# Eight ring places for the first weight granules, and S5's input weights asked for behind the sixth pair of modulation tiles

## The chip, the cores and the metric

One NeuronCore of a Trainium2 chip runs the whole program in one launch. The metric is the device time of one execution in microseconds (us).

## The reference

Two layers of a hybrid backbone over 256 context tokens and 256 latent tokens of width 1024, all in float32. What matters here is the beginning of each layer:

```python
def hybrid_layer(x, xc, c, c_ctx, p, cos, sin, ctx_out):
    mods = [m[:, None, :] for m in adaln(c, p)]     # silu(c) @ w_ada + b_ada, split in 6
    cmods = adaln(c_ctx, p)
    h = modulate(rmsnorm(x, p['norm1_g']), mods[0], mods[1])
    hc = modulate(rmsnorm(xc, p['norm1_g']), cmods[0], cmods[1])
    ua, ub, uatt, us5, ug = split_sections(h @ p['w_in'])
    ...
```

Four token mixers (RWKV-7, GLA, windowed attention, S5) follow, then their merge, the output projection, a second norm and a mixture of experts. `w_ada` is 1024 x 6144 per layer, `w_in` 1024 x 6688.

## The kernel before, in words

Weights come from HBM in *granules*: one granule is 128 partitions x 1024 float32, 512 KB, and holds eight 128 x 128 blocks. `gload` (L229) asks for one on SyncE's DMA queue and puts it in the next place of a ring, `self.ring`. In the first layer the ring has two places at first (pool `wp`) and four (with pool `wa`) while the modulation is computed. A place is asked for again only when its reader is done. `gsplit` (L239) loads a granule and splits it in two parts for the matmuls of high precision: ScalarE rounds it to float32r (tile `gs`), VectorE subtracts to get the rest (a second `gs`). `rowpair` (L266) does this for the two granules of S5's input weights.

The program is written as a sequence, and a scheduler deals its instructions out to the engines at build time; on each engine they then run in that order. So moving a call in the source can move the order on all engines for some distance around it.

In the first layer (`layer`, L1881) the beginning is this: x is loaded (`xi`, two requests of 1 MB), S5's small parameters (`s5_load`) on ScalarE's queue, S5's input weights by `rowpair` (L1916), and the norm (`norm1`): ScalarE squares and sums, VectorE works out the reciprocal root (tile `n`), both scale `xi`, TensorE transposes it into PSUM (`pb`), and ScalarE and VectorE copy it to `xr`. Then for each of eight column blocks k:

- `adaln` multiplies two granules of `w_ada` (k and 8 + k) with the conditioning vector (TensorE, `ada`), and VectorE adds the result to `mods`;
- `modcols` picks rows of `mods` out by a small matmul (`mps`), and VectorE makes scale and shift of it (`mc`, two instructions);
- `modulate` scales the two halves of `xr` (VectorE), ScalarE rounds to `hh`, VectorE subtracts to `hl`.

`s5` then begins with the projection of all eight blocks (matmuls `pa<-gs,hh` and `pa<-gs,hl`, 96 for the four quarters of time). The modulation columns 16 to 47 are multiplied later between other work, by `early`. PSUM bank A, which `ada` and `pa` share, has two buffers, so each waits for VectorE's use of the one before the last.

The tiles `yT` (L1895) hold the outputs of the four mixers, 128 x 1024 float32 each in the first layer; they are first written far into the layer. `kd` in DRAM is zeroed in part by two small DMAs (`zr`).

Of the kernel before, what the change touches and what calls it, by code (L numbers as in the profile page):

```python
# [9 lines left out]
F32 = mybir.dt.float32  # L10
# [167 lines left out]
class Net:  # L178
# [50 lines left out]
    def gload(self, src, pool=None):  # L229

        k, n = src.shape[1:]
        if pool is None:
            pool = self.ring[self.ri % len(self.ring)]
            self.ri += 1
        v = pool.tile([128, 1024], F32, tag="g", name="g")[:, 0:k * n].rearrange("p (k n) -> p k n", k=k)
        self.nc.sync.dma_start(v, src)
        return v

# [1642 lines left out]
    def layer(self, l, lo):  # L1881
        nc, tc, io = self.nc, self.tc, self.io
        nt = (512 - lo) // 128
        front = self.psum(f"pf{l}", A=2, X=1, B0=2, B1=2, C=1)
        self.ws = {s: ExitStack() for s in ("left", "right")}
        self.slots, self.early = [], []
        fs, hs, rs, bs = (ExitStack() for _ in range(4))

        def pool(es, name, side="left", bufs=1):
            return es.enter_context(tc.tile_pool(name=f"{name}{l}", bufs=bufs, side=side, reuse_waits="tile"))  # L1890
        wp = pool(fs, "wp", "right", 2)
        self.ring = [wp] * 2
        F = pool(fs, "F", "right")
        H = pool(hs, "H", "right")
        yT = [H.tile([128, 2, 512 - lo], F32, name=f"yT{i}") for i in range(4)]  # L1895
        h = [H.tile([128, 8, 512], F32R, name=n) for n in ("hh", "hl")]
        rm, p3, p4 = pool(rs, "rm"), pool(bs, "p3"), pool(bs, "p4")
        wx = pool(bs, "wx")

        self.mres = rm.tile([128, 512], F32, name="mres")  # L1900
        nc.gpsimd.memset(self.mres, 1.0)
        nc.gpsimd.memset(self.mres.rearrange("p (j t) -> p j t", t=64)[:, :, 0:1], 0.0)

        self.gp = [(F, f"a{i}") for i in range(4)] if l == 0 else [(self.xp, "x0"), (self.xp, "x1"), (F, "a0"), (F, "a1")]
        with ExitStack() as ns:
            tp = pool(ns, "n")
            mc = tp.tile([128, 2, 2, 8], F32, name="mc")
            mps = self.pc("mps")
            if l == 0:
                x = tp.tile([128, 4, D], F32, name="xi")  # L1910
                for s in range(2):
                    nc.sync.dma_start(x[:, 2 * s:2 * s + 2, :], io["x"][:, 2 * s:2 * s + 2, :])
                s5p = self.s5_load(l, p3)
                xr = tp.tile([128, 8, 512], F32, name="xr")
                xs = [x[:, t, :] for t in range(4)]
                s5w = self.rowpair(io["w_in_s5"][l, 0])  # L1916
                self.norm1(xs, xs, tp, lambda k, ps: (nc.vector.tensor_copy if k % 2 else nc.scalar.copy)(xr[:, k, :], ps))
                self.ring = self.ring + [pool(ns, "wa", bufs=2)] * 2
                for k in range(8):
                    self.adaln(0, [k, 8 + k])  # L1920
                    self.modcols(l, [k], mc, mps)
                    self.modulate(k, mc, h, xr[:, k, :], xr[:, k, :])
                self.ring = self.ring[0:2]
            else:
                self.modcols(l, range(8), mc, mps)
                s5p = self.s5_load(l, p3)
                gp, self.gp = self.gp, [(tp, "g0"), (F, "a0"), (tp, "g1"), (F, "a1")]
                s5w = self.rowpair(io["w_in_s5"][l, 0])
                self.gp = gp
                xn = [tp.tile([128, D], F32, name=f"xn{t}") for t in range(4)]  # L1930
                self.norm1(self.x, xn, tp, lambda k, ps: self.modulate(
                    k, mc, h, ps, tp.tile([128, 512], F32, tag="xm", bufs=2, name="xm")))
            s5p = self.s5_head(l, s5p, p3)
        todo = [(0, j) for j in range(16, 48)] + [(1, j) for j in range(16)] if l == 0 else [(1, j) for j in range(16, 48)]

        def some(n, bank="A"):
            for _ in range(min(n, len(todo))):
                a, j = todo.pop(0)
                self.adaln(a, [j], wx, bank)
        NB, C1, C2 = 24, 0, 3  # L1940

        def early(n):
            for _ in range(n):
                a, j = todo.pop(0)
                self.adaln(a, [j], wx, "X")
        early(32 if l else 0)
        self.bt = "B1"
        self.s5(l, h, s5w, yT[3], lo, p3, s5p)
        self.bt = "B0"
        early(0 if l else NB)  # L1950
        with ExitStack() as es:
            self.gla(l, h, yT[1], lo, pool(es, "p2"))
        st = self.rwkv_in(l, h, lo, rm, p4, lambda: None)
        us = ExitStack()
        up = pool(us, "up", "right")
        self.rwkv_first(l, st, up)
        with ExitStack() as es:
            self.attn(l, h, yT[2], lo, pool(es, "p1"))
        bs.close()
        m = 1024 // (512 - lo)  # L1960
        acc = [F.tile([128, m, 512 - lo], F32, tag=f"a{i}", name="acc") for i in range(8 // m)]
        acc = [a[:, i, :] for a in acc for i in range(m)]
        with ExitStack() as es:
            p0, p = pool(es, "p0"), pool(es, "p5")
            self.gp = [(p, f"g{i}") for i in (0, 1, 2, 2)] if l == 0 else self.gp[0:2] + [(p, "g0"), (p, "g1")]
            self.rwkv_units(l, st, yT[0], p0, p, 4 if l else 3)
            for n, i in enumerate((1, 3, 2)):
                self.merge(l, i, h, yT[i], acc, lo, n == 0, p, lambda: some(C1), self.pa if l == 0 else None)
        us.close()
        rs.close()  # L1970
        if l == 0:
            self.xp = self.xs.enter_context(tc.tile_pool(name="xp", bufs=1, reuse_waits="tile"))
        self.bt = "B0"
        wo = pool(self.ws["left"], "wo", bufs=4)
        self.eopen(l, "left", EB[l][0])
        with ExitStack() as es:
            p = pool(es, "p6")
            if l == 0:
                wx = pool(es, "wy", bufs=2)
            self.gp = [(p, f"g{i}") for i in range(4)] if l == 0 else self.gp[0:2] + [(p, "g0"), (p, "g1")]  # L1980
            self.merge(l, 0, h, yT[0], acc, lo, False, p, lambda: some(C2, "B1"), self.pb)
        if l == 0:
            self.xload()
        w = [self.blocks([self.wtile(io["w_out"][l, n, :, k:k + 4], wo) for k in (0, 4)]) for n in range(2)]
        self.eahead(l)
        hs.close()
        with ExitStack() as es:
            mo = pool(es, "mo")
            ex = self.tail(l, lo, acc, mo, w)
            fs.close()  # L1990
            front.__exit__(None, None, None)
            self.eopen(l, "right", EB[l][1])
            self.eahead(l)
            self.slots += [wo] * 4
            self.moe(l, lo, ex)
        self.ws["right"].close()
        self.ws["left"].close()
# [22 lines left out]
```

## Time and profile before

| | |
|---|---|
| median of 3 runs | 2438.41 us (2432.42 to 2440.38) |
| the profiled execution | 2436.24 us, its span 2434.5 us |
| TensorE busy | 2233.6 us (92% of the span) |
| VectorE busy | 1220.8 us (50%) |
| ScalarE busy | 657.7 us (27%) |
| mean granted TensorE clock | 0.959 of full speed |

The span runs from the first to the last instruction; the execution's own time has 1.7 us around it. Times in the rows below are counted from the span's start. A line number such as L272 can be that of a helper that records every matmul, so rows are told apart by the names of the tiles, written as result <- inputs.

### The profile page before, as it was taken

How to read it: one execution, taken by the hardware profiler on the slowest of the kernel's cores; microseconds unless marked ns; L12 is line 12 of the kernel's file. 1: busy time of each engine (PE TensorE's matmuls, PEld its weight loads, DVE VectorE, ACT ScalarE, POOL GpSimd, SP SyncE). 2: the span in 40 equal slices, each digit the busy share in tenths (PEclk: the TensorE clock that was granted, in tenths of full speed). 3: DMA queues.
4: the chain of work that ended last, by engine and by line, in shares of the span. 5: the costliest groups of instructions: out<-in, count | busy, mean ns of one | idle time of the engine just before them, and what ended most of it. 6: DMA issues, size and time to landing. Idle time of an engine off the chain costs nothing. (4 is left out here: it accounts for less than half of the span.)

```text
span 2434.5 us, 38729 instructions
## 1 busy us (share of the span) xinstructions
PE 2233.6 (92%) x15351; PEld 1302.5 (54%) x15351; DVE 1220.8 (50%) x3229; ACT 657.7 (27%) x1217; POOL 316.0 (13%) x351
## 2 busy tenths in 40 slices
PE   5999989999999799999999799999999799999996
PEld 4876757677764333333333486767778433333332
DVE  6685567754433454332333668858755432222222
ACT  3254443322211111111111325543333111111111
POOL 0000000000000043323333100100000012222211
PEclk9997989999999799999999799989999799999998
DMA  7342111115470799999997244412228499999994
GB/s 249 124 137 78 62 44 41 51 58 185 147 242 20 274 419 417 380 399 381 378 379 305 77 152 157 136 59 78 65 91 302 180 375 418 419 419 419 419 419 206
DMA packets 149436, 557.42 MB, mean 229 GB/s; under 512 B 38484, under 2 KB 69588, under 8 KB 98820
## 3 DMA queue, kind: packets, MB, share of 16 engines
q1 hardware_dynamic: 139088, 542.66, 58.2%
q10 hardware_dynamic: 5556, 5.94, 0.8%
q0 software_dynamic: 4608, 6.30, 0.8%
q8 instruction: 124, 2.03, 0.3%
q14 instruction: 60, 0.49, 0.1%
HBM read 558.56 MB, written 6.75 MB: 232 GB/s over the span
## 5 line engine op out<-in xcount | busy, mean ns | idle before, releaser
L272 PE MATMUL pa<-hh,gs 128*128 128x512 f32 (+2 forms) x1440 | 421.3, 367 | 9.2 <-ACT sg L275 5.2
L272 PEld LDWEIGHTS pa<-hh,gs 128*128 128x128 f32 (+1 forms) x1440 | 254.4, 190 | 68.4 <-issue 15.1
L272 PE MATMUL pd<-w,hT 128*64 128x512 f32 x1024 | 278.3, 599 | 1.4 <-ACT hT L275 1.4
L272 PE MATMUL pgate<-w,xT 128*64 128x512 f32 x1024 | 262.6, 602 | 0.0
L272 PE MATMUL pa<-hl,gs 128*128 128x512 f32 (+2 forms) x720 | 254.8, 367 | 0.0
L272 PE MATMUL pup<-w,xT 128*64 128x512 f32 x1024 | 250.5, 592 | 0.0
L278 POOL TENSOR_TENSOR ta<-ta,mb 128x512 f32<-128x512 f32 x93 | 125.0, 1351 | 726.9 <-ACT ta L275 726.8
L278 DVE TENSOR_TENSOR gs<-g,gs 128x1024 fp32r<-128x1024 f32 (+1 forms) x106 | 128.2, 1211 | 111.2 <-PE pa L272 82.5
L275 ACT ACTIVATE gs<-g 128x1024 fp32r<-128x1024 f32 (+1 forms) x106 | 110.5, 1045 | 190.9 <-PE pa L272 140.0
L272 PEld LDWEIGHTS pup<-w,xT 128*64 128x64 f32 x1024 | 81.3, 137 | 146.5 <-issue 144.8
L272 PE MATMUL py<-yp,oT 128*128 128x512 f32 x384 | 128.3, 437 | 31.2 <-ACT ta L275 23.1
L272 PEld LDWEIGHTS pd<-w,hT 128*64 128x64 f32 x1024 | 81.7, 136 | 138.1 <-issue 130.3
L272 PEld LDWEIGHTS pgate<-w,xT 128*64 128x64 f32 x1024 | 75.7, 138 | 148.9 <-issue 137.5
L272 PEld LDWEIGHTS pa<-hl,gs 128*128 128x128 f32 (+1 forms) x720 | 138.0, 192 | 27.2 <-issue 7.9
L272 PEld LDWEIGHTS py<-yp,oT 128*128 128x128 f32 x384 | 62.1, 190 | 122.2 <-ACT ta L275 44.5
L288 DVE SCALAR_TENSOR_TENSOR hd<-hd,pgate 128x512 f32<-128x512 f32 x32 | 22.0, 688 | 208.0 <-ACT hd L275 207.9
L278 POOL TENSOR_TENSOR x<-x,ta 128x512 f32<-128x512 f32 x93 | 123.8, 1337 | 3.8
L278 DVE TENSOR_TENSOR tm<-py,mb 128x512 f32<-128x512 f32 x99 | 66.7, 687 | 88.3 <-PE py L272 88.3
L272 PE MATMUL pa<-gs,hh 128*128 128x256 f32 x480 | 107.6, 319 | 2.4 <-DVE gs L278 1.8
L1660 DVE TENSOR_TENSOR hd<-hd,pup 128x512 f32<-128x512 f32 x32 | 22.0, 687 | 174.4 <-PE pup L272 174.4
L275 ACT ACTIVATE yp<-pd,at 128x512 fp32r<-128x512 f32 x64 | 44.0, 688 | 241.7 <-PE pd L272 241.7
L288 DVE SCALAR_TENSOR_TENSOR yp<-pd,at,yp 128x512 fp32r<-128x512 f32 x64 | 47.7, 745 | 122.6 <-ACT yp L275 122.6
(505 smaller groups left out, 3408.1 us busy)
## 6 DMA issues: line engine op xcount, KB each, us to landing
w<-in_w_g SPq DMA_DIRECT2D x128, 1024.0 KB, 11.6
w<-in_w_d SPq DMA_DIRECT2D x128, 1024.0 KB, 13.3
w<-in_w_u SPq DMA_DIRECT2D x128, 1024.0 KB, 12.1
g<-in_w_ada SPq DMA_DIRECT2D x96, 512.0 KB, 3.9
g<-in_w_in_gate SPq DMA_DIRECT2D x64, 512.0 KB, 3.8
g<-in_w_in_rwkv SPq DMA_DIRECT2D x16, 512.0 KB, 3.9
wb<-in_w_branch SPq DMA_DIRECT2D x64, 128.0 KB, 3.6
w<-in_w_out SPq DMA_DIRECT2D x8, 1024.0 KB, 6.4
```

Of the source, the lines that this page charges most:

```text
L272: self.nc.tensor.matmul(out, lhsT, rhs, start=start, stop=stop, skip_group_check=True)
L275: self.nc.scalar.activation(out, in_, f, **kw)
L278: (eng or self.nc.vector).tensor_tensor(out, a, b, op)
L288: self.nc.vector.scalar_tensor_tensor(out, a, s, b, op0=op0, op1=op1)
L1660: last = nc.vector.tensor_tensor(hd, hd, pu, OP.mult).ins
```

## The change

Granules can now be put in a place of any pool and tag. While the first layer's modulation is computed the ring has eight places, the four of before and four in pool H with the tags y0 to y3. The four `yT` tiles are made after `s5_head`, with the same tags, so each takes the memory of one of these places. S5's input weights are asked for inside the loop, ahead of k = 6, where twelve modulation granules have been asked for.

```diff
--- before.py
+++ after.py
@@ -232,7 +232,8 @@
         if pool is None:
             pool = self.ring[self.ri % len(self.ring)]
             self.ri += 1
-        v = pool.tile([128, 1024], F32, tag="g", name="g")[:, 0:k * n].rearrange("p (k n) -> p k n", k=k)
+        pool, tag = pool if isinstance(pool, tuple) else (pool, "g")
+        v = pool.tile([128, 1024], F32, tag=tag, name="g")[:, 0:k * n].rearrange("p (k n) -> p k n", k=k)
         self.nc.sync.dma_start(v, src)
         return v
 
@@ -1892,7 +1893,6 @@
         self.ring = [wp] * 2
         F = pool(fs, "F", "right")
         H = pool(hs, "H", "right")
-        yT = [H.tile([128, 2, 512 - lo], F32, name=f"yT{i}") for i in range(4)]
         h = [H.tile([128, 8, 512], F32R, name=n) for n in ("hh", "hl")]
         rm, p3, p4 = pool(rs, "rm"), pool(bs, "p3"), pool(bs, "p4")
         wx = pool(bs, "wx")
@@ -1913,10 +1913,12 @@
                 s5p = self.s5_load(l, p3)
                 xr = tp.tile([128, 8, 512], F32, name="xr")
                 xs = [x[:, t, :] for t in range(4)]
-                s5w = self.rowpair(io["w_in_s5"][l, 0])
                 self.norm1(xs, xs, tp, lambda k, ps: (nc.vector.tensor_copy if k % 2 else nc.scalar.copy)(xr[:, k, :], ps))
-                self.ring = self.ring + [pool(ns, "wa", bufs=2)] * 2
+
+                self.ring = self.ring + [pool(ns, "wa", bufs=2)] * 2 + [(H, f"y{i}") for i in range(4)]
                 for k in range(8):
+                    if k == 6:
+                        s5w = self.rowpair(io["w_in_s5"][l, 0])
                     self.adaln(0, [k, 8 + k])
                     self.modcols(l, [k], mc, mps)
                     self.modulate(k, mc, h, xr[:, k, :], xr[:, k, :])
@@ -1931,6 +1933,8 @@
                 self.norm1(self.x, xn, tp, lambda k, ps: self.modulate(
                     k, mc, h, ps, tp.tile([128, 512], F32, tag="xm", bufs=2, name="xm")))
             s5p = self.s5_head(l, s5p, p3)
+        yT = [H.tile([128, 2 * (512 - lo)], F32, tag=f"y{i}", name=f"yT{i}").rearrange("p (z n) -> p z n", z=2)
+              for i in range(4)]
         todo = [(0, j) for j in range(16, 48)] + [(1, j) for j in range(16)] if l == 0 else [(1, j) for j in range(16, 48)]
 
         def some(n, bank="A"):
```

SyncE's queue (`SP`) at the start of the program. Names: `xi` is x, `in_w_in_s` S5's input weights, `in_w_ada` the modulation weights, `zr` the zeros for `kd`, `in_w_in_gla` and its like the weights of GLA. Before:

```order
L1912 DMA xi<-in_x 128x2048 x2
L236 DMA g<-in_w_in_s 128x1024 x2
L236 DMA g<-in_w_ada 128x1024 x2
L1102 DMA kd<-zr 112x256
L236 DMA g<-in_w_ada 128x1024 x6
L1103 DMA kd<-zr 112x256
L236 DMA g<-in_w_ada 128x1024 x10
L236 DMA g<-in_w_in_glaa 128x256
```

And now:

```order
L1912 DMA xi<-in_x 128x2048 x2
L237 DMA g<-in_w_ada 128x1024 x12
L237 DMA g<-in_w_in_s 128x1024 x2
L237 DMA g<-in_w_ada 128x1024 x4
L1103 DMA kd<-zr 112x256
L1104 DMA kd<-zr 112x256
L237 DMA g<-in_w_ada 128x1024
L237 DMA g<-in_w_in_glaa 128x256
```

S5's two requests moved behind twelve of the modulation, both zero writes behind all sixteen, and the first two requests for later modulation columns, which stood among the eighteen of before, behind the zero writes.

VectorE's row in the modulation loop, where the splits of S5's weights (`gs`) now stand:

```order
L279 TENSOR_TENSOR mods<-ada,mods 128x128 x2
L289 SCALAR_TENSOR_TENSOR mc<-mps,prm_62 128x2
L1355 COPY mc<-mps 128x2
L279 TENSOR_TENSOR hl<-xr,hh 128x512
L286 TENSOR_SCALAR xr<-xr,mc 128x256 x2
L279 TENSOR_TENSOR mods<-ada,mods 128x128
L279 TENSOR_TENSOR gs<-g,gs 128x1024
L279 TENSOR_TENSOR hl<-xr,hh 128x512
L289 SCALAR_TENSOR_TENSOR mc<-mps,prm_62 128x2
L1355 COPY mc<-mps 128x2
L279 TENSOR_TENSOR gs<-g,gs 128x1024
L286 TENSOR_SCALAR xr<-xr,mc 128x256 x2
```

Before, the same two instructions stood in one row near VectorE's start, among S5's parameters:

```order
L283 TENSOR_SCALAR nci<-s5ci 128x256
L278 TENSOR_TENSOR dg<-cst,dd 16x128
L278 TENSOR_TENSOR gs<-g,gs 128x1024 x2
L278 TENSOR_TENSOR sm_475<-s5lr,s5dt 128x16
L278 TENSOR_TENSOR sm_476<-s5li,s5dt 128x16
```

They moved from behind the first loads to the middle of the loop. TensorE's row had seventeen granules (eight matmuls each) ahead of S5's first matmul; now that part of it ends so:

```order
L273 MATMUL ada<-g,cT 32x128 x8
L273 MATMUL mps<-cst,mods 128x12
L273 MATMUL ada<-g,cT 32x128 x16
L273 MATMUL mps<-cst,mods 128x12
L273 MATMUL ada<-g,cT 32x128 x16
L273 MATMUL pa<-gs,hh 128x256 x2
L273 MATMUL pa<-gs,hl 128x256
```

Sixteen granules stand ahead of S5 now; the seventeenth moved behind the projection. From there to about the 440th row of TensorE, which is the end of GLA, the order of S5, GLA and the first RWKV projections differs in many places; behind that it is the same.

## Rows read from the trace of the kernel before

**Rows 1.** The page: busy time, share of the span and instructions of each engine.

```profile
PE 2233.6 (92%) x15351; PEld 1302.5 (54%) x15351; DVE 1220.8 (50%) x3229; ACT 657.7 (27%) x1217; POOL 316.0 (13%) x351
```

**Rows 2.** Stretches: us, engines' busy us (instructions), granted clock, DMA share, GB/s.

```profile
18.00:50.00 32.00, 21.75 (x301) 16.67 (x302) 27.94 (x136) 13.44 (x26) 1.93 (x3) 0.87 0.82 288
24.00:32.00 8.00, 5.58 (x49) 4.57 (x46) 5.63 (x38) 3.47 (x6) 0.00 (x0) 1.00 0.95 351
31.50:50.50 19.00, 14.66 (x230) 11.04 (x228) 17.55 (x70) 6.35 (x11) 1.93 (x3) 0.77 0.83 291
17.60:50.50 32.90, 22.65 (x312) 16.80 (x302) 28.81 (x138) 13.97 (x27) 1.93 (x3) 0.86 0.81 284
60.00:180.00 120.00, 116.25 (x1158) 91.89 (x1158) 94.01 (x267) 47.20 (x92) 0.49 (x5) 1.00 0.40 127
186.00:202.00 16.00, 15.38 (x112) 11.45 (x113) 9.31 (x20) 1.72 (x3) 2.09 (x4) 0.50 0.16 58
```

**Rows 3.** Timeline of TensorE: start us, us, what, [idle before <- releaser].

```profile
27.70 1.03 PE L272 MATMUL ada<-g,cT 128*32 128x128 f32 x10 [0.20 <-DMA g<-in_w_ada]
...
28.66 3.27 PE L1387 MATMUL pb<-cst,xi 128*128 128x128 f32 x16
...
49.50 1.08 PE L272 MATMUL ada<-g,cT 128*32 128x128 f32 x16 [0.28 <-DMA g<-in_w_ada]
...
50.51 0.84 PE L272 MATMUL pa<-gs,hh 128*128 128x256 f32 x2
...
88.55 0.64 PE L272 MATMUL ada<-g,cT 128*32 128x128 f32 x16
```

**Rows 4.** Waits of SyncE's DMA queue, 0 to 60 us: us, times, longest.

```profile
SPq L236 <- PE ada L272: 14.7, 10, 3.5
...
SPq L236 <- DMA s5dt<-in_s5dt: 2.2, 1, 2.2
```

**Rows 5.** Timeline of all engines, 43.7 to 44.9 us.

```profile
43.77 0.29 DVE L278 TENSOR_TENSOR mods<-ada,mods 128x128 f32<-128x128 f32 x1
...
44.12 0.60 PE L272 MATMUL mps<-cst,mods 128*128 128x12 f32 x2 [0.38 <-DVE mods L278]
...
44.77 0.15 DVE L288 SCALAR_TENSOR_TENSOR mc<-mps,prm 128x2 f32<-128x2 f32 x1
```

**Rows 6.** Timeline of VectorE, 0 to 60 us.

```profile
17.63 0.29 DVE L283 TENSOR_SCALAR nci<-s5ci 128x256 f32<-128x256 f32 x1 [5.22 <-DMA s5ci<-in_s5ci]
...
18.06 2.34 DVE L278 TENSOR_TENSOR gs<-g,gs 128x1024 fp32r<-128x1024 f32 x2
...
22.49 0.16 DVE L285 TENSOR_SCALAR n<-n 128x4 f32<-128x4 f32 x1
...
25.67 1.41 DVE L283 TENSOR_SCALAR xi<-xi,n 128x1024 f32<-128x1024 f32 x2
...
31.52 1.29 DVE L1917 COPY xr<-pb 128x512 f32<-128x512 f32 x2 [1.85 <-PE pb L1387]
...
35.69 0.73 DVE L285 TENSOR_SCALAR xr<-xr,mc 128x256 f32<-128x256 f32 x2
...
36.33 0.49 DVE L278 TENSOR_TENSOR mods<-ada,mods 128x128 f32<-128x128 f32 x2
...
37.11 0.69 DVE L278 TENSOR_TENSOR hl<-xr,hh 128x512 fp32r<-128x512 f32 x1
...
37.72 0.15 DVE L288 SCALAR_TENSOR_TENSOR mc<-mps,prm 128x2 f32<-128x2 f32 x1
...
46.38 0.17 DVE L278 TENSOR_TENSOR u<-scr 128x16 f32<-128x16 f32 x1
...
46.47 0.29 DVE L278 TENSOR_TENSOR t<-cf,s5br 128x128 f32<-128x128 f32 x1
```

**Rows 7.** Timeline of TensorE, 150 to 260 us.

```profile
158.51 0.66 PE L826 MATMUL pc<-cst,ke 128*128 128x128 f32 x4 [0.80 <-DVE ke L278]
...
186.62 0.66 PE L272 MATMUL pb<-sc,v 128*64 128x128 f32 x2 [2.35 <-DVE sc L278]
```

## The prediction

> **What bounds the kernel now.** I read the page's engine line first: TensorE is busy 92% of the span [rows 1], and from 60 to 180 us it works 116.25 of 120 us [rows 2]. So the program is one chain of matmuls, and what a change of the first 50 us is worth is the time at which the dense matmuls begin. The timeline of TensorE shows that moment: S5's input projection starts at 50.51 us, right behind a modulation granule whose transfer came last, at 49.50 [rows 3]. From there on TensorE hardly waits, so an earlier start is passed on almost whole, unless a later stretch loses it.
>
> Three things could hold that start. The windows show the transfers: 288 GB/s from 18 to 50 us, against 351 GB/s in the 8 us where they stand closest [rows 2]. The waits of the DMA-issuing queue say why: 14.7 us in ten waits for TensorE to read a ring place free, and 2.2 us for a small load of ScalarE's queue [rows 4]. VectorE itself is busy 28.81 of the 32.9 us from 17.6 to 50.5, and 17.55 of the last 19 [rows 2]. And there are round trips: a VectorE add at 43.77, the selection matmul at 44.12, VectorE's answer at 44.77 [rows 5].
>
> **The change, part by part.** *Eight places.* The first eight modulation granules need no place given back. By bytes: 288 GB/s x 32 us = 9.2 MB moved from 18 to 50 us; two granules of 0.52 MB that S5 does not need (the first two of the columns that come after it) are now asked for behind all that it does need, which leaves 8.2 MB; at 351 GB/s this is 23.3 us, so the last granule could be there at 41.3 and S5 could start at 42.4, with 1.1 us for its matmuls [rows 3]. Transfers alone would allow 8.1 us.
>
> *S5's weights moved.* Their two requests go past twelve modulation requests in SyncE's queue; their two ScalarE copies and two VectorE subtractions go behind the fourth to sixth modulated tiles. The subtractions take 2.34 us in all, from 18.06 [rows 6]. Before, they stood where VectorE had little else that was ready; the wait for s5ci in front of them, until 17.63, stays, since nothing ahead of it moves. They come back in the busy stretch, between tiles 3 and 6, at the same price. No engine saves work by it.
>
> *VectorE's chain is the new limit.* From 17.6 us to S5's first matmul VectorE has 32.9 - 28.81 = 4.1 us of idle time to lose. In the new order 18 small operations of S5's coefficients (scr, pw, t, bb, u and cf) stand behind the last add that S5's first matmul waits for, instead of ahead of it. Seven have 128 columns, 0.29 us long but 0.2 apart, the others mostly 16, 0.09 from one start to the next [rows 6]: 7 x 0.2 + 11 x 0.11 = 2.6 us. With no wait left the start would be 50.5 - 4.1 - 2.6 = 43.8, which is behind the 42.4 of the transfers. So VectorE, not the transfers, sets the bound.
>
> *Waits that the new order has of its own.* VectorE works strictly in the order shown. (a) The early mods, mc and mods rows now stand in front of the norm's short chain (n), which before ran from 22.49 to 25.6. TensorE needs 1.0 us from an add to mc [rows 5], with 0.45 to 0.65 us of other work between: I count 0.5, 0.55 and 0.35 us, 1.4 in all. So the norm ends near 25.1 instead of 25.6, although VectorE reaches it with the split's 2.34 us no longer ahead of it. (b) For the fourth and fifth tiles the selection's answer stands directly behind the adds, with 0.2 us between: 0.8 us each, 1.6 together. (c) For the first copies from PSUM and for one split (hl, which waits for ScalarE's 0.6 us copy) 0.5 us. Sum 3.5 us. The transposes come out better: before, they were held until 28.66 by a granule that landed at 27.70 [rows 3]; now half of them can run while the second half of x is scaled. That is how VectorE's first copy can move from 31.52 to about 28.6, and it is inside the idle time already counted.
>
> So S5 starts at 43.8 + 3.5 = 47.3 us, 3.2 us earlier. Check forward from 28.6: the four copies, fourteen scalings, six hl, nine adds, five pairs of mc, two splits and four small ones up to that add are 16.1 us by the starts in [rows 6] (a copy 0.6, a pair of scalings 0.64, hl 0.61, an add 0.2, a split 1.13; two mc 0.15 [rows 5]), and the 2.1 us of (b) and (c) give 46.8. The two agree within half a microsecond.
>
> *One granule goes behind.* Sixteen, not seventeen, modulation granules are multiplied ahead of S5. The other now lies in TensorE's dense stretch: +0.64 us at full clock [rows 3].
>
> *The rest.* The yT tiles take the four places once their granules are read, long before the first write; the place of a tile in memory costs nothing. S5's two zero writes of kd go behind the modulation requests, where S5's whole projection, 50.51 us and after, covers them: kd is read only by the quarters behind it. Uncovered they would hold those loads by one transfer. In the second layer the ring stays as it was.
>
> Sum: -3.2 + 0.6 = **-2.6 us**. The profiled execution took 2436.24, which gives 2433.6; it lies 2.2 under the median of the three runs, so against the median of 2438.41 I expect 2435.8, a change of 0.1%. A measurement of this kernel can tell about 0.3%, 7.3 us, from no change; the three runs themselves lie 8 us apart. The bounds of this part are 0 (VectorE's waits grow as fast as the others go) and -6.1 (none of the 3.5 us comes).
>
> **A rule against the trace.** SyncE's ten waits for TensorE in the ring [rows 4] are gaps that repeat. The Trainium skill, Perfetto Trace Analysis, section Identifying Performance Opportunities, says that consistent bubbles can mean that there is not enough room for the next tile to be allocated. By that rule more places close the gaps, which is the first rival below; the row that speaks against a full closing is VectorE's 17.55 of 19 us [rows 2].
>
> **The rivals.**
> 1. *The waits go whole.* The new order's own waits are covered and S5 starts at 43.8: -6.7 + 0.6 = -6.1, 2432.3. For it: TensorE's and SyncE's waits in the ring are the longest of the stretch [rows 3, 4]. Against it: VectorE's order, in which mc stands right behind the adds.
> 2. *A cold stretch goes.* From the S5 quarters to the end of GLA the order on TensorE is dealt anew. Before, a wait of 2.35 us for VectorE's sc at 186.62 [rows 7] was followed by 16 us in which the granted clock was 0.50, that is 1.2 GHz [rows 2]. Sixteen granule matmuls take 1.08 us at 0.50 and 0.64 at 1.00 [rows 3]; by that ratio the 15.38 us of work would take 9.2. If wait and cold stretch vanish, 2.35 + 6.2 = 8.5 us: -11.1 in all, 2427.3. For it: in the new order matmuls of the next projection stand among GLA's short ones. Against it: VectorE has as much to do there as before.
> 3. *Slower: a new cold stretch.* The same mixing puts wide projection matmuls behind short ones that wait for VectorE. If TensorE waits over some 2.4 us in a row there, as at 186.62, and the 16 us at 0.50 that follow hold wide matmuls, which take twice as long at half the clock, this costs 2.35 + 8 = 10.4 us: +7.8 in all, 2446.2. It decides from a wait of that length; a shorter one, 0.80 us at 158.51 [rows 7], left the clock at 1.00 [rows 2]. For it: 94 of 120 us on VectorE from 60 to 180 [rows 2]. Against it: the old order has this wait already.
> 4. *The places do nothing.* SyncE's requests also wait for completion counts that they share with ScalarE's small loads (s5dt, 2.2 us) [rows 4]; in the new queue six of the first twelve granules do, one of S5's two and two of the last four. If one of these loads comes late, in-order SyncE holds all behind it, and S5 starts as before: +0.6, 2439.0.
>
> **How the numbers follow.** Forecast 0.36, waits whole 0.26, cold stretch gone 0.16, new cold stretch 0.12, no effect 0.10. Faster by over 0.3% is the third case, a third of the second (0.09; it lies 1.2 us short of the line, and the runs scatter more than that) and 0.05 of the first: 0.30. Slower by over 0.3% is nearly all of the fourth: 0.11. The rest, 0.59, is no change that can be told. The range leaves out the far halves of the two cold cases and reaches from 2426.5 to 2445.
>
> **What would show it.** In the profile after: S5's first matmul between 46 and 48.5 us; SyncE's waits for TensorE in the first 60 us far under 14.7; VectorE busy over 95% from its first copy, near 28.6, to S5's start. Wrong if S5 starts before 44 (VectorE did not hold it) or after 50, or if the granted clock of the GLA stretch differs from before, which would outweigh all of the front.

## The result, and the profile after

The first comparison, four executions of each kernel: 2414.80 us for the change (2407.67 to 2422.09) against 2439.39 before (2432.42 to 2447.06), a ratio of 0.9899 with a 95% interval from 0.9856 to 0.9942. That is 24.6 us, over nine times what I forecast, and 2414.80 lies outside my range. Two later comparisons, with twelve executions of the change in each beside 35 and 29 of the kernel before, did not give this size again:

| what ran | median, us | before, beside it | ratio (95%) |
|---|---|---|---|
| the change, second time | 2427.37 | 2436.34 | 0.9974 (0.9941 to 1.0007) |
| the change, third time | 2422.68 | 2432.23 | 0.9945 (0.9919 to 0.9971) |

In the later comparisons the ratio, with its interval, is an estimate of its own and differs a little from the quotient of the two medians.

All 116 later executions of the kernel before lie between 2413.0 and 2446.6 us (mean 2433.4), all 24 of the change between 2409.6 and 2443.9 (mean 2425.7). The difference of the means is -7.7 us, with 4.3 us of uncertainty from the scatter (95%). So there are two things to explain: where some 8 us come from, where 2.6 were forecast, and why one kernel's executions lie over 30 us apart.

The profiled execution of the change took 2422.09 us, the slowest of its four. Its page, as [rows 1]:

```profile
PE 2226.5 (92%) x15351; PEld 1299.3 (54%) x15351; DVE 1222.0 (50%) x3229; ACT 657.0 (27%) x1217; POOL 316.6 (13%) x351
```

The numbers of instructions are the same. TensorE's 7.1 us less of busy time go with a mean granted clock of 0.962 in this execution, 0.959 in the one before. Stretches of the change, as [rows 2] (us, engines' busy us, granted clock, DMA share, GB/s; the third starts at VectorE's first copy and ends at S5's first matmul):

```profile
18.00:50.00 32.00, 23.36 (x278) 18.47 (x279) 28.14 (x120) 15.47 (x28) 1.96 (x3) 0.77 0.78 285
24.00:32.00 8.00, 7.90 (x81) 6.25 (x76) 7.10 (x35) 4.53 (x7) 0.00 (x0) 1.00 0.94 359
28.96:48.05 19.09, 13.28 (x190) 10.26 (x188) 18.08 (x53) 8.24 (x13) 1.96 (x3) 0.66 0.68 247
60.00:180.00 120.00, 115.98 (x1148) 89.55 (x1148) 93.18 (x264) 46.87 (x90) 0.60 (x6) 1.00 0.43 143
186.00:202.00 16.00, 16.00 (x148) 11.59 (x146) 13.15 (x29) 4.03 (x6) 0.38 (x2) 0.79 0.50 166
```

TensorE's timeline of the change, as [rows 3] and [rows 7]:

```profile
48.05 0.84 PE L273 MATMUL pa<-gs,hh 128*128 128x256 f32 x2
...
179.48 0.43 PE L273 MATMUL pb<-sc,v 128*64 128x128 f32 x2 [1.71 <-DVE sc L279]
...
265.79 0.91 PE L273 MATMUL psc<-ar,bk 64*128 64x192 f32 x4
```

VectorE's first copy, as in [rows 6], and the waits of SyncE's queue up to 60 us, as [rows 4]:

```profile
28.96 1.29 DVE L1916 COPY xr<-pb 128x512 f32<-128x512 f32 x2
```

```profile
SPq L237 <- PE ada L273: 8.3, 4, 5.6
...
SPq L237 <- DMA s5dt<-in_s5dt: 2.6, 1, 2.6
```

The front came nearly as forecast: S5's first matmul moved from 50.51 to 48.05 us, and VectorE is busy 18.08 of the 19.09 us before it. But the lead then grew. The first psc matmul (RWKV's first units, behind S5's quarters and GLA) moved by 13.5 us, from 279.34 in the trace of before to 265.79. Between the two lies the stretch in which the scheduler deals TensorE's order anew. There the granted clock was 0.50 from 186 to 202 us before [rows 2], and is 0.79 now. The question was whether that belongs to the change.

### The profile page after: what moved, and what is told of

It reads as the page before. It is cut to its first block, busy times and chain, and to the rows that moved or that the text cites. A ratio compares the mean times of both kernels' runs of the same rounds, so it can differ in the third digit from the quotient of the medians.

```text
span 2420.3 us, 38728 instructions
## 1 busy us (share of the span) xinstructions
PE 2226.5 (92%) x15351; PEld 1299.3 (54%) x15351; DVE 1222.0 (50%) x3229; ACT 657.0 (27%) x1217; POOL 316.6 (13%) x351
```

## The experiments

*Theory 1*: the front gives 2.5 us, and the new order of the S5 and GLA stretch some 8 to 11 us more, by a shorter low clock. *Rivals*: the early start of S5 alone; the room in the ring; the place of yT in memory; chance.

One table first. Each profile is one execution, whose time stands in the first column. "Way" is the time from S5's first matmul to the first psc matmul, "idle" the part of the way in which TensorE was not busy, "clock" the granted clock from 150 to 200 and from 200 to 250 us.

| kernel profiled | execution, us | S5, us | psc, us | way, us | idle, us | clock |
|---|---|---|---|---|---|---|
| before | 2436.24 | 50.51 | 279.34 | 228.8 | 7.5 | 0.85, 0.84 |
| only yT moved (before's order) | 2435.93 | 50.76 | 280.26 | 229.5 | 7.6 | 0.82, 0.84 |
| control (before's order) | 2443.01 | 50.91 | 280.44 | 229.5 | 8.1 | 0.86, 0.90 |
| before, wait filled | 2429.62 | 48.86 | 267.49 | 218.6 | 6.8 | 1.00, 1.00 |
| the same, second time | 2431.07 | 50.99 | 275.54 | 224.6 | 4.9 | 0.90, 0.93 |
| the change | 2422.09 | 48.05 | 265.79 | 217.7 | 4.5 | 0.93, 1.00 |
| second time | 2426.83 | 48.69 | 276.48 | 227.8 | 5.8 | 0.83, 0.90 |
| third time | 2441.19 | 47.55 | 274.31 | 226.8 | 5.9 | 0.81, 0.95 |
| five places (the change's order) | 2426.53 | 46.80 | 267.86 | 221.1 | 4.8 | 0.90, 0.97 |
| places alone | 2445.28 | 47.75 | 274.49 | 226.7 | 6.5 | 0.82, 0.94 |
| S5's weights at k = 5 | 2421.71 | 47.22 | 274.88 | 227.7 | 8.4 | 0.85, 0.88 |
| S5's weights moved alone | 2414.30 | 48.53 | 264.53 | 216.0 | 3.8 | 0.90, 1.00 |
| the change, wait filled | 2430.47 | 48.47 | 268.57 | 220.1 | 2.1 | 0.93, 0.97 |
| the same, second time | 2422.81 | 47.98 | 265.00 | 217.0 | 4.4 | 1.00, 1.00 |

Two things can be read from it. Behind psc, where the order is the same in both kernels, the four executions with the change's order take 2150.4 to 2166.9 us (mean 2158.1) and the three with before's 2155.7 to 2162.6 (mean 2158.4): on the mean the gain lies ahead of psc, and single executions differ widely behind it. On the way TensorE is idle for 4.5 to 5.9 us with the change's order and for 7.5 to 8.1 with before's. So some 2.5 us of waiting go in all four profiles. The rest of the way, its busy time, is what differs from one execution of the same order to the next. The way before, with the change, and with the change the third time (us, TensorE's busy us, granted clock, DMA share, GB/s):

```profile
50.51:279.34 228.83, 221.29 (x1877) 0.93 0.33 105
48.05:265.79 217.74, 213.21 (x1893) 0.97 0.34 113
47.55:274.31 226.76, 220.88 (x1893) 0.94 0.33 108
```

**Only yT moved.** Before, with the yT tiles made behind `s5_head` in the tags of pool H, as in the change, and nothing else.

```diff
-        yT = [H.tile([128, 2, 512 - lo], F32, name=f"yT{i}") for i in range(4)]
...
+        yT = [H.tile([128, 2 * (512 - lo)], F32, tag=f"y{i}", name=f"yT{i}").rearrange("p (z n) -> p z n", z=2)
+              for i in range(4)]
```

> Four ring places and S5's weights first, as before; only the yT tiles are made later, in pool H by tag. The order on every engine is that of before. Theory 1 (the S5 and GLA stretch's new order makes most of the gain): S5's first matmul at 50.5 us, granted clock low again near 186 to 202 us, time within 0.3% of before. Rival (the place of yT in memory makes a part of it): under 2430 us with before's order.

Measured: 2436.67 us against 2434.36, ratio 1.0017 (0.9987 to 1.0047). The place in memory is worth nothing. Its profile is a second execution of before's order, with the same wait of 2.35 us and a way 0.7 us from before's.

**Places alone.** The change with S5's weights asked for first again.

```diff
+                s5w = self.rowpair(io["w_in_s5"][l, 0])
                 self.norm1(xs, xs, tp, ...
...
-                    if k == 6:
-                        s5w = self.rowpair(io["w_in_s5"][l, 0])
```

> Eight places, but S5's weights asked for first, as before. From TensorE's 372nd matmul on the order is that of the change, since the scheduler deals S5's quarters and GLA out the same way. Theory 1 (that order makes the gain): 2410 to 2422 us, with the granted clock from 150 to 260 us like the change's, wherever S5 starts. Rival A (the early start of S5 alone counts): the time follows S5's first matmul, each us of it one us against before, so with S5 at 45 to 49 us 2434 to 2438. Rival B (moving S5's weights makes the gain): no change from before.

Measured: 2429.03, ratio 0.9979 (0.9953 to 1.0005). Theory 1 missed: the order behind the 372nd matmul is the change's, but the profile's clock is 0.82 in 150 to 200 us and the way 226.7. Rival A named 2434 to 2438, which is missed too, but its figures started from a before of 2439: by its rule, the 2.8 us that S5 starts earlier, the 2434.36 beside this kernel give 2431.6, and the interval allows that. It allows rival B's no change as well. Of the front it says something definite: S5 starts at 47.75, with the places but without the move. Its timeline has the change's wait of 1.71 us for sc, and 2.4 us later one for a granule that the change's profile has not:

```profile
180.16 0.43 PE L273 MATMUL pb<-sc,v 128*64 128x128 f32 x2 [1.71 <-DVE sc L279]
...
182.60 1.03 PE L273 MATMUL ada<-g,cT 128*32 128x128 f32 x10 [0.84 <-DMA g<-in_w_ada]
```

**Five places.** The change with `range(1)` for `range(4)` in the ring's line; every engine's order is the change's.

> The change with five ring places in place of eight: every engine has the change's own order from first to last, only requests wait longer for a place. Theory 1: the change's time plus what the front loses, at most 2.5 us, so 2413 to 2421. Rival (the room of eight places counts by itself): S5 at 50 us or later and about 2436.

Measured: 2425.47, ratio 0.9957 (0.9927 to 0.9986), S5 at 46.80. That misses theory 1's 2413 to 2421 and both figures of the rival. Its SyncE queue, 0 to 60 us:

```profile
SPq L237 <- PE ada L273: 20.6, 10, 4.0
...
SPq L237 <- DMA s5dt<-in_s5dt: 2.7, 1, 2.7
```

20.6 us of waits for places, where the change has 8.3 and before 14.7 [rows 4], and yet the earliest start of S5 of all. More room than five places brought S5 no earlier start. But one more thing differs. With eight places GpSimd (POOL in the rows) clears GLA's tiles sb and sc while VectorE scales a tile of the modulation, and that pair of scalings takes 1.93 us:

```profile
39.24 1.93 DVE L286 TENSOR_SCALAR xr<-xr,mc 128x256 f32<-128x256 f32 x2
39.61 0.96 POOL L855 MEMSET sb<- 128x1024 f32 x1 [28.89 <-PE ada L273]
40.50 1.13 POOL L858 MEMSET sc<- 64x512 f32 x2
```

With five places the clearing comes behind S5's start, and the pair takes 0.73 us as it does before [rows 6]:

```profile
38.76 0.73 DVE L286 TENSOR_SCALAR xr<-xr,mc 128x256 f32<-128x256 f32 x2
...
47.00 0.96 POOL L855 MEMSET sb<- 128x1024 f32 x1 [35.86 <-DMA g<-in_w_in_glaa]
```

In all five profiles with the change's order and eight places the pair beside the clearing is this long (1.93 us in four, 2.22 in one). The 1.2 us are about the difference between 48.05 and 46.80.

**S5's weights one step earlier** (`if k == 5`).

> The change with S5's weights asked for one step of the loop earlier (k = 5). S5's first matmul should stand within 1 us of the change's 48.05, but from there to the first RWKV projections the scheduler gives a third order, neither that of before nor that of the change. Theory 1: the time goes by that order: it differs from the change by as much as the low-clock stretches between 76 and 300 us differ, 0 to 11 us either way (2405 to 2430). Rival A (the front counts): within 3 us of the change.

Measured: 2429.07, ratio 0.9990 (0.9968 to 1.0012). S5 starts at 47.22, 3.3 us ahead of before, and the time cannot be told from before's. It lies in theory 1's 2405 to 2430, a range too wide to decide much. The way is 227.7: this order has waits for sc of its own, the one below and one of 1.44 us at 212.16.

```profile
194.20 0.66 PE L273 MATMUL pb<-sc,v 128*64 128x128 f32 x2 [1.36 <-DVE sc L279]
```

**S5's weights moved alone.** The kernel before with the two requests moved to k = 6, four places.

```diff
-                s5w = self.rowpair(io["w_in_s5"][l, 0])
...
                 for k in range(8):
+                    if k == 6:
+                        s5w = self.rowpair(io["w_in_s5"][l, 0])
```

> S5's weights asked for ahead of k = 6 as in the change, but with the four ring places of before; the yT tiles as before. TensorE's order up to S5's start is that of the change, and then a fourth one of its own. If the room in the ring holds the front, S5's first matmul stands at 50 us or later; if the place of S5's weights in the queues makes the front's gain, at 47 to 48.5. Theory 1: the whole time then goes by the low-clock stretches from 76 to 300 us, within 0.4% of before; rival (the early start counts): 2 to 3 us under before.

Measured: 2430.75 against 2436.34, ratio 0.9982 (0.9961 to 1.0002). S5 starts at 48.53 with four places. Both expectations for the whole time, within 0.4% of before and 2 to 3 us under it, fit the interval. So either half of the change, the places or the move, brings S5 to about 48; together they bring no more. They do it by different orders on VectorE: its first copy stands at 31.17 us with the places alone, with the splits of S5's weights near its start as before, and at 28.30 with the move alone, where TensorE then waits 1.01 and 0.71 us for granules shortly before S5 (at 45.72 and 47.52). The way is the shortest of all, 216.0, but the profiled execution, 2414.30, is also the fastest of the twelve of this kernel. One way says little of a kernel.

**The change again, twice.** No edit.

> The change itself once more, with more executions beside more of the kernel before. Theory 1 (the front gives 2.5 us, the S5 and GLA stretch some 8 to 11 us of low clock; what came above that in the first comparison was the scatter of single executions, which differ by up to 30 us from one another): 9 to 15 us under the median of before in the same call. Rival (the whole first difference is the change's own): 20 to 26 us under it.

> The change a third time. If the executions of one kernel scatter by chance about a mean that is 7 to 9 us under before's (as the five-place kernel, which has the same order, and the second look at the change had it): 5 to 12 us under the median of before in this call. If the first comparison had the change's true size: 20 us or more.

Measured: 9.0 us under before, a hair under the 9 to 15 named, and 9.6 us. The rival of 20 us or more is out for these runs. The second and third profile show why one profile had misled me. The order is the same and so is the wait for sc, but here the clock went low and stayed so. The change, third time, granted clock (last three columns: clock, DMA share, GB/s) and the wait:

```profile
180.00:185.00 5.00, 4.34 (x26) 0.63 0.17 66
185.00:190.00 5.00, 5.00 (x50) 0.50 0.05 13
190.00:195.00 5.00, 5.00 (x25) 0.50 0.70 211
195.00:200.00 5.00, 5.00 (x53) 0.50 0.02 2
```

```profile
180.36 0.43 PE L273 MATMUL pb<-sc,v 128*64 128x128 f32 x2 [1.70 <-DVE sc L279]
```

In the first profile of the change this wait of 1.71 us ended at 179.48, and the clock was low for a far shorter time:

```profile
180.00:185.00 5.00, 4.80 (x71) 1.00 0.02 8
185.00:190.00 5.00, 5.00 (x48) 0.88 0.62 186
190.00:195.00 5.00, 5.00 (x40) 0.50 0.32 97
195.00:200.00 5.00, 5.00 (x55) 0.94 0.47 167
```

So the order does not fix the clock. Of four executions with the change's order two gained 8 and 12 us on the way against before's 229 (217.7 and 221.1), and two gained 1.5 and 2.5. In these two some 2 us of saved waiting are all that is left.

**Before, its wait filled.** Nothing moves. Seven matmuls of constants are added to TensorE's order ahead of the matmul that waited at 186.62 [rows 7], one before the sixteen ada matmuls there and six behind them. They write a half of a PSUM tile that nothing reads. All other rows of all engines stay as they were. The extra line stands in GLA's loop over heads (`gla_dir`), behind the products of ki and qd.

```diff
+                if lo == 0 and d == 0 and h == 3:
+                    for _ in range(7):
+                        self.mm(ps[:, 256:512], ident, self.cst[:, 0:256], True, True)
```

> The kernel before, with seven extra matmuls of constants (128 x 256, into a half of a PSUM tile that nothing reads) in TensorE's order ahead of the matmul that waited at 186.62 us; every other instruction on every engine stands where it did. They add work that nothing needs. Theory 1 (the wait for VectorE's sc brings the low clock behind it): the granted clock from 186 to 202 us is near 1.00, the first psc matmul comes 6 to 9 us earlier than the 279.3 us of before, and the median is 4 to 9 us under before. Rival (the clock falls there for another reason, the many narrow matmuls): the clock stays at 0.50, psc within 1.5 us of before, and the median is the same.

> The filled kernel before a second time, since one profile of the change had the low clock from 180 to 200 us and another had little of it, so one profile of the filled kernel could be chance too. Theory (filling the wait for sc lifts the clock): the granted clock from 150 to 250 us is again 0.95 or more, the way from S5's first matmul to the first psc matmul takes 217 to 222 us as in its first profile (218.6), against 229 in the three profiles with before's order, and the median is 4 to 9 us under before. Rival (chance): 229 us, the clock at 0.50 near 190 us, and the median of before.

Measured: 2428.06 against 2436.34, ratio 0.9970 (0.9946 to 0.9995), and 2426.79 against 2437.30, ratio 0.9971 (0.9951 to 0.9991). Work that nobody needs makes the kernel some 6 us faster (means of 24 executions against 116: -5.7, uncertain by 2.2). Lines fitted through the executions of each kernel, time against mean granted clock, give 2431.9 us for this one and 2431.6 for before at a clock of 0.960: what it gained went with a higher clock. TensorE's timeline of the first, the place of the old wait:

```profile
182.76 0.64 PE L272 MATMUL ada<-g,cT 128*32 128x128 f32 x16
183.34 2.86 PE L272 MATMUL pb<-cst 128*128 128x256 f32 x12
186.12 0.32 PE L272 MATMUL pb<-sc,v 128*64 128x128 f32 x1
```

In the first profile the clock is 1.00 throughout and the way 218.6. In the second the theory is only half met: the time is lower by 7 us by the ratio and 10.5 by the medians, where 4 to 9 was named, but the clock from 150 to 250 us is 0.90 and 0.93 where 0.95 was named, and the way 224.6 where 217 to 222 was. The clock is low, but for a shorter time.

```profile
180.00:185.00 5.00, 4.92 (x58) 0.89 0.69 210
185.00:190.00 5.00, 5.00 (x26) 0.50 0.31 105
190.00:195.00 5.00, 4.67 (x38) 0.93 0.01 3
195.00:200.00 5.00, 5.00 (x76) 1.00 0.29 105
```

The same stretch with before's order (only yT moved):

```profile
180.00:185.00 5.00, 5.00 (x69) 0.73 0.68 202
185.00:190.00 5.00, 2.65 (x27) 0.50 0.30 108
190.00:195.00 5.00, 5.00 (x34) 0.50 0.00 0
195.00:200.00 5.00, 5.00 (x32) 0.50 0.32 105
200.00:205.00 5.00, 4.25 (x102) 0.72 0.23 83
```

```profile
182.51 1.88 PE L273 MATMUL pb<-qd,ki 32*64 32x64 f32 x32
...
187.75 0.66 PE L273 MATMUL pb<-sc,v 128*64 128x128 f32 x2 [2.35 <-DVE sc L279]
```

The wait began at 187.75 - 2.35 = 185.40, but the clock was down before 185, among GLA's narrow matmuls. So the wait does not always start the low clock. In these two profiles what differs is the end of the low clock: 1.00 again at 195 in the filled kernel, not before 200 in this one.

**Control.** The same seven matmuls, with `d == 1`, so they run some 36 us behind the wait (at 223.60 in its profile). Otherwise before's order, but for two neighbouring small copies on VectorE that change places.

> A control of the filled kernel before: the same seven matmuls of constants, but some 30 us later in TensorE's order, between the last matmuls of GLA and the next projection, where TensorE waits for nothing over 0.4 us. Otherwise before's order. Theory (filling the wait for sc lifts the clock): here that wait of 2.35 us stays, the granted clock is again at 0.50 somewhere from 185 to 202 us, and the median is within 4 us of before. Rival (the extra matmuls, or any shift of what follows, change the clock): as fast as the filled kernel, 6 to 10 us under before.

Measured: 2438.67 against 2432.23, ratio 1.0016 (0.9984 to 1.0048). By the medians that is 6.4 us slower, where within 4 was named; the interval holds both. Here the seven matmuls take 4.81 us of TensorE's time, with no long wait to hide in. The wait:

```profile
187.55 0.66 PE L272 MATMUL pb<-sc,v 128*64 128x128 f32 x2 [2.35 <-DVE sc L278]
```

The way is before's 229.5. By the means of the executions it is 8.5 us slower than the filled kernel (uncertain by 5.5). So extra matmuls, or a shift of what follows, do not by themselves make the gain; their place in the wait does.

**The change, its wait filled.** Five such matmuls in the PSUM tile of the modulation granule j = 35, around the wait of 1.71 us.

```diff
+            if l == 0 and j == 35:
+                for _ in range(5):
+                    self.mm(pf[:, 128:384], self.ident, self.cst[:, 0:256], True, True)
```

> The change, with five such extra matmuls around TensorE's wait of 1.71 us for VectorE's sc at 179.48 us; TensorE's order is otherwise the change's, VectorE has one add of mods and one sc swapped. Theory 1: the low clock from 189 to 196 us goes, psc comes 3 to 4 us earlier than the change's 265.8 us, and the median is 2 to 4 us under the change's in this call. Rival: the low clock there has another cause, and nothing changes beyond 1 us.

> The filled change a second time, beside the change in one call. If filling the one wait is worth something: 2 to 5 us under the change, and 9 to 14 under before. If its first lead of 4 us over the change was scatter: within 2 us of the change.

Measured: 2423.46 (ratio to before 0.9947, 0.9920 to 0.9973) and 2426.60 (0.9977, 0.9952 to 1.0003), against 2427.37 and 2422.68 for the change beside them. The first lead over the change, 3.9 us as theory 1 had it, turned round in the second, which is 3.9 us behind and misses both of its expectations. In the first profile the clock was still low (0.50 from 190 to 195 us) and psc came at 268.57, not 3 to 4 us before 265.8; in the second it was 1.00 from 150 to 250 us. The two ways are short, 220.1 and 217.0, but no gain on the whole program can be told, and no version tried here is faster than the change. What did shrink is the scatter: a standard deviation of 6.0 us over 24 executions against 10.1.

## Why the prediction was wrong

**"S5 starts at 47.3 us, 3.2 us earlier": right, a little large.** S5's first matmul stands at 48.05, 48.69, 47.55, 48.47 and 47.98 in five profiles with the change's order and eight places, and at 50.51, 50.76, 50.91, 48.86 and 50.99 in five with before's: 2.3 us earlier by the means. What the sum did not have is the long pair of scalings beside GpSimd's clearing, 1.2 us in the change's profile. Less that, 48.05 becomes 46.85, which is the prediction's check forward (46.8) and the start with five places (46.80). That the clearing makes the pair long is read from the profiles; no run moved it by itself.

**"VectorE's chain is the new limit": supported.** VectorE is busy 18.08 of 19.09 us (95%) from its first copy, at 28.96 (forecast: near 28.6), of which 1.2 us are the long pair. S5 does not start earlier with eight places (48.1 by the mean of the five profiles) than with five (46.80). SyncE's waits for TensorE did fall, as forecast (14.7 to 8.3 us), but the five-place kernel has 20.6 us of them and the earliest start, so they were not what held S5. The rule of the Trainium skill that I set against the trace, on consistent bubbles (Perfetto Trace Analysis, section Identifying Performance Opportunities), speaks of gaps on the engine that should be saturated. I read it for SyncE's queue, which only issues transfers, and these rows say nothing against the rule itself.

**"The places do nothing" and "the waits go whole"** (rivals 4 and 1): both wrong as put. S5 starts neither as before nor at 43.8. The places are not needed for it, though: the move alone gives the start at 48.53.

**"An earlier start is passed on almost whole, unless a later stretch loses it": this is the step that failed.** I priced the dealt-anew stretch between S5's first matmul and the end of GLA at zero in the sum, and left its clock to two rivals at 0.16 and 0.12. The way through it is 228.8, 229.5 and 229.5 us with before's order, and 217.7, 227.8, 226.8 and 221.1 with the change's: 5.9 us shorter by the means. With the front's 2.3 this makes 8.2, near the 7.7 measured. The means of three and four ways are uncertain by some 5 us or more, but the whole program says the same: 7.7 less the front's 2.3 leaves 5.4, uncertain by 4.3. So the term was not 0 but between 5 and 6 us of gain by either count, more than twice the front. It has two parts. TensorE's idle time on the way is 2.5 us shorter by the means, in all four profiles: the new order has other and shorter waits, 1.71 us for sc in place of 2.35 among them. Its busy time is 3.5 us shorter by the means, in two of the four, and that goes with the granted clock (0.97 against 0.93 in the rows of the way above). My "Wrong if ... the granted clock of the GLA stretch differs from before, which would outweigh all of the front" is what happened in these two.

**Rival 2, "a cold stretch goes": half right.** Its price was 8.5 us on this stretch (15.38 us at its ratio of 0.64 to 1.08 are 9.1, not 9.2, which changes little). The two good executions paid 8 and 12, the two others 2. Its mechanism was that the wait for sc vanishes. It did not: it is 1.71 or 1.70 us in all of the change's profiles without filling, and low clock came both with it and without. The filled kernels show that shortening this idle time is worth time in before's order. That it is the cause of the change's share by the clock is argued, not shown, and stays open.

**Rival 3, "a new cold stretch": did not come.** No comparison has the change slower than before. Its condition, and rival 2's, was a wait like the 2.35 us one. The clock does not go by that length alone: it was 0.50 behind a wait of 1.70 us in the change's third profile, and down before the wait began with only yT moved.

**The size of the first comparison.** Across the 116 executions of the kernel before, time and mean granted clock go together (correlation -0.95; the fitted line has 1.9 us for each 0.001). On such lines the two kernels differ by 4.3 us at a clock of 0.960 (2431.6 and 2427.4), and the mean clock of the later executions is 0.9591 before and 0.9609 with the change, which is the other 3.4. This fits the parts above: the front's 2.3 and some 2 us of saved waiting at equal clock, and the rest by the clock. The four first executions of the change had 0.962 to 0.969, mean 0.9655, where the line of the later ones gives 2416.8, near the 2414.80 measured. If four are drawn from the 24 later ones of the change and four from 99 of before, a difference of 24.6 us or more comes in about 1 case of 100. So most of the first size was favourable clock in few executions; whether something else helped (the comparisons ran on different chips) stays open. Against the later runs my 2435.8 is still wrong: the change lies near 2426, just under the range's low end, partly since the median I started from, 2438.4, was 4 us over the 2434.7 of the 116.

## What to carry to other kernels

When an edit makes a scheduler deal a stretch anew, the stretch needs a term of its own in the sum, with the clock in it. Here it was worth more than twice the front that the edit was about, by the means. Before a difference of 1% is explained, the executions of one kernel should be set side by side: here they span 1.4%, and one profile showed a gain that two others of the same kernel did not. A wait of TensorE in a stretch of narrow matmuls can be tested directly, by matmuls that nobody reads put into it and, as a control, elsewhere. And a change of buffers can move the work of an engine that is nearly idle: here GpSimd's clearing came to lie beside VectorE's scalings, and 1.2 us of the front went with it.

## What was unexpected of the hardware

The same order with the same waits gets a different clock from one execution to the next. At attention's end the change (second time) and its filled form have one order and the same waits (0.78, 0.29, 0.24, 0.47 and 1.28 us). Behind the last of them, the change, second time: its timeline, then the 17 us from there (granted clock the third number from the end):

```profile
326.93 0.49 PE L273 MATMUL pa<-hh,gs 128*128 128x512 f32 x1 [1.28 <-ACT gs L276]
327.35 0.91 PE L273 MATMUL psc<-ar,bk 64*128 64x192 f32 x4
```

```profile
327.00:344.00 17.00, 16.46 (x65) 1.00 0.33 103
```

The filled change, the same:

```profile
319.02 0.50 PE L273 MATMUL pa<-hh,gs 128*128 128x512 f32 x1 [1.28 <-ACT gs L276]
319.45 1.64 PE L273 MATMUL psc<-ar,bk 64*128 64x192 f32 x4
```

```profile
319.00:336.00 17.00, 16.98 (x36) 0.51 0.25 72
```

One went on at 2.4 GHz, the other at 1.2, where the four psc matmuls take 1.64 us in place of 0.91 and 36 matmul records fill the time of 65. The Trainium skill, TensorE: Matmul & The Clock Gate, section What's actually happening, says that the number of matmuls at the low clock at a kernel's start varies from run to run of one kernel; in these traces it varies 320 us into the program too. The section puts the cost of that one warm-up below 1% of a typical kernel's span. What the 116 executions of before show is not a warm-up's cost but the scatter of whole executions: 33.6 us of 2433, 1.4%.

And the clock can be low while TensorE is busy. In the trace of before it fell again, from 222 to 236 us, where GLA's products of 32 or 64 rows or columns (ki, qd, sc) alternate with a few wide ones:

```profile
222.00:236.00 14.00, 14.00 (x59) 0.52 0.01 2
```

TensorE is busy 14.00 of 14.00 us there, and its last wait, at 216.23, was 0.32 us long. The low level is the 1.2 GHz one. Busy time is no sign that the clock is granted.
